# Interleaved rotary embedding: the first position of tile 0 leaves in 4 KB fp32 rows over the Activation queue

## Chip, cores, metric

The kernel runs on one core of one Trainium2 chip. The metric is device time in microseconds (us), the median of several executions. The kernel before takes 317.48 us (317.40 to 317.68, 6 runs). "Span" is the stretch that the profile covers, about 1.8 us less than the time.

## The reference

```python
# x: (8, 2048, 16, 64) fp32; cos, sin: (2048, 32) fp32
x1, x2 = x_pairs[..., 0], x_pairs[..., 1]      # even and odd elements of each head
out1 = x1 * cos - x2 * sin
out2 = x1 * sin + x2 * cos
out  = np.stack([out1, out2], axis=-1).reshape(x.shape)   # fp32
```

67.1 MB come in, 67.1 MB go out, and there are three operations on each element. Nearly everything about the time is a question of moving bytes.

## The kernel before

Each of the 8 batches is one tile: 128 partitions, 16 positions in each, 1024 elements per position. Loads and stores are issued by the Pool engine, and they change the data type on the way (a cast): fp32 in HBM, bf16 on the chip. One row (one partition of one tile) is 64 KB in HBM and 32 KB on the chip.

```python
P = 128; K = S // P; KP = 8; HEAD = 2; TAIL = 4       # K = 16; NX = NO = 3 buffers
x_t = x.rearrange("b (p k) h d -> b p k (h d)", p=P, k=K)
...
def load(b, k0=0):                       # fp32 -> bf16 in the DMA
    ...
    nc.gpsimd.dma_start(out=xs[b][:, k0:], in_=x_t[b, :, k0:])

def store(b, k1=K):                      # bf16 -> fp32 in the DMA
    nc.gpsimd.dma_start(out=out_t[b, :, :k1], in_=os[b][:, :k1])

def rotate(b, k0, k1):                   # three VectorE instructions; in short:
    ...
    o = x * c_tab;   x = x * s_tab;   o = o + x_with_neighbours_swapped

# start: positions 0 and 1 of tile 0 in fp32 over the SP and Activation queues,
# then cos and sin, then
load(0, HEAD); load(1)
...                                      # ACT casts the head, DVE builds the tables
load(2)
for b in range(B):
    os[b] = opool.tile([P, K, HD], bf16, name="ot")
    for k0 in range(0, K, KP):
        rotate(b, k0, k0 + KP)
    if b + NX < B:
        load(b + NX)
    store(b, K if b < B - 1 else K - TAIL)
...                                      # last 4 positions: cast on ACT, stored by SP
```

## Time and profile before

| what | value | where |
|---|---|---|
| time, span | 317.48 us, 315.7 us | the runs, the page |
| HBM traffic | 134.7 MB, 427 GB/s over the span | totals of the page |
| DVE (VectorE) busy | 212.8 us, 67% | busy line |
| DMA busy | 9 tenths in every slice but the last | slice rows |
| one load and one store together | 38.6 us for 16.78 MB, 434 GB/s | timeline |

From the page of the kernel before: the span, the busy line of DVE (us, share of the span, instructions), the slice rows (one digit for a 40th of the span, in tenths), and the DMA queues. The Pool queue is q0, SP's is q1, Activation's is q10; the columns are packets, MB, share of 16 engines' span.

```profile
span 315.7 us, 146 instructions
...
DVE 212.8 (67%) x51; ACT 6.9 (2%) x4; POOL 8.8 (3%) x20
...
DVE  0009999999999999619992299913999049990000
...
DMA  9999999999999999999999999999999999999996
...
q0 software_dynamic: 2304, 98.04, 97.0%
q1 hardware_dynamic: 432, 2.88, 2.4%
q10 hardware_dynamic: 288, 0.79, 0.6%
HBM read 67.63 MB, written 67.11 MB: 427 GB/s over the span
```

DVE has holes, the DMA engines have none. The DMA row is what limits the kernel.

Two pieces of the timeline of the kernel before follow (start us, us, engine, line, operation, output<-input, and in brackets how long the engine was idle and what ended that). The first piece is the end of tile 0, the second shows where tile 4 and tile 5 begin.

```profile
47.48 4.42 DVE L81 TENSOR_TENSOR ot<-ot,xt 128x8192 bf16<-128x8192 bf16 x1
51.82 4.42 DVE L75 TENSOR_TENSOR ot<-xt,c_tab 128x8192 bf16<-128x8192 bf16 x1
52.20 0.53 POOL L57 DMA_DIRECT2D xt<-in_x_dram  x1 [25.93 <-DVE ot L81]
52.72 0.54 POOL L60 DMA_DIRECT2D out_dram<-ot  x1
...
140.95 4.42 DVE L75 TENSOR_TENSOR ot<-xt,c_tab 128x8192 bf16<-128x8192 bf16 x1 [9.53 <-DMA out_dram<-ot]
...
179.53 4.42 DVE L75 TENSOR_TENSOR ot<-xt,c_tab 128x8192 bf16<-128x8192 bf16 x1 [11.98 <-DMA out_dram<-ot]
```

DVE waits until a store has left its output buffer, so these starts mark when a store landed: every 38.6 us, in which one load and one store passed.

Below the profile's views lie the records of the single DMA packets. I read from them, for the Pool queue, how far apart one engine's packets start. A packet is one row here, and the step is the time from one engine's packet start to its next. This is my own table (mean over 16 engines), not a view of the profile:

```
kernel before, Pool queue                step from packet to packet, us
loads 1 and 2 (64 KB read, 32 KB written)        2.412
last packet of load 3 -> first of store 0        3.168   (once only)
store 0 (32 KB read, 64 KB written)              2.41
later changes between load and store             2.43 to 2.45
```

65,536 bytes x 16 engines / 2.412 us is 434.7 GB/s. Loads and stores have the same step, and a load next to a store gains nothing: an engine works at the speed of the fp32 side, whether that side is read or written. The number agrees with the Trainium skill, "DMA: Bandwidth & Descriptors", section "Where 436 GB/s comes from", which gives 435.2 GB/s for the 16 ports together.

### The profile page before, as it was taken

Reading aid. Unit: us, or ns where it says so; the run is one execution under the profiler, and the core shown is the slowest. Engines: PE = TensorE matmul, PEld = TensorE weight load, DVE = VectorE, ACT = ScalarE, POOL = GpSimd, SP = SyncE. Lnnn points to the kernel's source line nnn. Section 1 sums busy time; section 2 is a strip of 40 time slices with the busy share of each in tenths; the row PEclk is TensorE's granted clock in tenths of the full one; section 3 lists DMA queues with packets and bytes.
Section 4 is the critical chain, followed back from the end, with each engine's and each line's share of the span. In section 5 each row is a group of like instructions: output and inputs, shape, how many; then the busy total and the mean of one; then the engine's idle time right before and its main releaser. Section 6 shows DMA issues by size and latency. Waiting matters only on the chain.

```text
span 315.7 us, 146 instructions
## 1 busy us (share of the span) xinstructions
DVE 212.8 (67%) x51; ACT 6.9 (2%) x4; POOL 8.8 (3%) x20
## 2 busy tenths in 40 slices
DVE  0009999999999999619992299913999049990000
ACT  2100000000000000000000000000000000000400
POOL 1000001000100100100001000000000000000000
DMA  9999999999999999999999999999999999999996
GB/s 269 212 246 203 199 212 253 199 199 237 361 465 332 199 257 407 399 332 262 203 399 440 357 199 199 482 448 266 199 316 415 399 399 523 407 399 457 423 434 280
DMA packets 3024, 101.71 MB, mean 322 GB/s; under 512 B 336, under 2 KB 336, under 8 KB 848
## 3 DMA queue, kind: packets, MB, share of 16 engines
q0 software_dynamic: 2304, 98.04, 97.0%
q1 hardware_dynamic: 432, 2.88, 2.4%
q10 hardware_dynamic: 288, 0.79, 0.6%
HBM read 67.63 MB, written 67.11 MB: 427 GB/s over the span
## 4 chain that ended last, share of the span: by engine, by line
another core or an unknown queue 61%; DMA 16%; DVE 9%; ACT 1%; issue 0%; POOL 0%; ACTq 0%
DMA out_dram<-ot 16%; DVE xt L76 3%; DVE ot L81 3%; DVE ot L75 3%; ACT xt L117 1%; DVE c_tab L100 0%; POOL xt L57 0%; ACTq L116 0%; ACT ot L116 0%; ACTq L117 0%
## 5 line engine op out<-in xcount | busy, mean ns | idle before, releaser
L75 DVE TENSOR_TENSOR ot<-xt,c_tab 128x8192 bf16<-128x8192 bf16 x16 | 70.7, 4420 | 45.8 <-DMA out_dram<-ot 45.7
L81 DVE TENSOR_TENSOR ot<-ot,xt 128x8192 bf16<-128x8192 bf16 x16 | 70.8, 4425 | 0.5
L76 DVE TENSOR_TENSOR xt<-xt,s_tab 128x8192 bf16<-128x8192 bf16 x16 | 70.8, 4425 | 0.5
L98 DVE CAST s_tab<-xt 128x512 bf16<-128x512 f32 x1 | 0.5, 454 | 23.8 <-DMA xt<-in_sin_dram 23.8
L57 POOL DMA_DIRECT2D xt<-in_x_dram x8 | 4.4, 547 | 161.4 <-DVE ot L81 137.4
L60 POOL DMA_DIRECT2D out_dram<-ot x8 | 4.3, 535 | 113.8 <-DVE ot L81 113.8
L116 ACT COPY ot<-ot 1x1 bf16<-1x1 bf16 x1 | 0.2, 193 | 286.6 <-DMA out_dram<-ot 286.6
L117 ACT CAST xt<-ot 128x4096 f32<-128x4096 bf16 x1 | 3.6, 3604 | 0.0
L96 ACT CAST xt<-xt 128x2048 bf16<-128x2048 f32 x1 | 1.9, 1897 | 0.0
L96 ACT ACT_TABLE_LOAD x1 | 1.3, 1283 | 5.7 <-DMA xt<-in_x_dram 5.7
L100 DVE CAST c_tab<-xt 128x1024 bf16<-128x1024 f32 x1 | 0.7, 683 | 0.0
L99 DVE TENSOR_SCALAR s_tab<-xt 128x512 bf16<-128x512 f32 x1 | 0.4, 442 | 0.0
L133 POOL MEMSET const-float32-0.0<- 128x1 f32 x1 | 0.1, 98 | 0.2 <-issue 0.2
L133 POOL MEMSET const-bfloat16-1.0<- 128x1 bf16 x1 | 0.1, 101 | 0.0
L133 POOL MEMSET const-float32-1.0<- 128x1 f32 x1 | 0.1, 98 | 0.0
L133 POOL MEMSET const-uint8-127<- 128x1 uint8 x1 | 0.1, 98 | 0.0
## 6 DMA issues: line engine op xcount, KB each, us to landing
xt<-in_x_dram POOLq DMA_DIRECT2D x7, 4096.0 KB, 42.8
out_dram<-ot POOLq DMA_DIRECT2D x1, 6144.0 KB, 28.0
xt<-in_x_dram POOLq DMA_DIRECT2D x1, 3584.0 KB, 22.8
out_dram<-xt SPq DMA_DIRECT2D x1, 2048.0 KB, 15.5
xt<-in_x_dram ACTq DMA_DIRECT2D x1, 512.0 KB, 5.0
xt<-in_x_dram SPq DMA_DIRECT2D x1, 512.0 KB, 4.9
xt<-in_sin_dram ACTq DMA_DIRECT2D x1, 256.0 KB, 22.7
xt<-in_cos_dram SPq DMA_DIRECT2D x1, 256.0 KB, 18.3
```

The lines of the kernel that those rows point to most:

```text
L57: nc.gpsimd.dma_start(out=xs[b][:, k0:], in_=x_t[b, :, k0:])
L60: nc.gpsimd.dma_start(out=out_t[b, :, :k1], in_=os[b][:, :k1])
L75: nc.vector.tensor_tensor(out=rows(op), in0=rows(xp), in1=tab(c_tab), op=mult)
L76: nc.vector.tensor_tensor(out=rows(xp), in0=rows(xp), in1=tab(s_tab), op=mult)
L81: nc.vector.tensor_tensor(out=o3, in0=o3, in1=x_swap, op=add)
L96: nc.scalar.copy(out=xs[0][:, :HEAD], in_=pre[:, :HEAD])
L98: nc.vector.tensor_copy(out=s2[:, :, 0], in_=sin_sb)
L99: nc.vector.tensor_scalar_mul(s2[:, :, 1], sin_sb, -1.0)
L100: nc.vector.tensor_copy(out=c_tab.rearrange("p k (i j) -> p (k i) j", j=2), in_=cos_sb.to_broadcast([P, K * D2, 2]),)
L116: nc.scalar.copy(out=os[B - 2][:1, 0, :1], in_=os[B - 1][:1, K - 1, :1])
L117: nc.scalar.copy(out=tail[:, :TAIL], in_=os[B - 1][:, K - TAIL :])
L133: nc = _bacc.Bacc("TRN2", target_bir_lowering=False, num_devices=1)
```

## The change

The intent: until 82 us, when the first packet of store 0 starts, the DMA engines only load. If the first results are ready early, a part of store 0 could leave under those loads, and store 0 would be shorter. The Activation queue is idle at that time. It gets rows that are fp32 already: ACT does the cast first.

```diff
+    LEAD = 1
+    lead = consts.tile([P, LEAD, HD], fp32)
...
-    def store(b, k1=K):
-        nc.gpsimd.dma_start(out=out_t[b, :, :k1], in_=os[b][:, :k1])
+    def store(b, k0=0, k1=K):
+        nc.gpsimd.dma_start(out=out_t[b, :, k0:k1], in_=os[b][:, k0:k1])
...
-            for k0 in range(0, K, KP):
-                rotate(b, k0, k0 + KP)
+            cuts = [0, KP, K]
+            if b == 0:
+                rotate(b, 0, HEAD)
+                nc.scalar.copy(out=lead, in_=os[b][:, :LEAD])
+                nc.scalar.dma_start(out=out_t[b, :, :LEAD], in_=lead)
+                cuts = [HEAD, KP, K]
+            for k0, k1 in zip(cuts, cuts[1:]):
+                rotate(b, k0, k1)
             if b + NX < B:
                 load(b + NX)
-            store(b, K if b < B - 1 else K - TAIL)
+            store(b, LEAD if b == 0 else 0, K if b < B - 1 else K - TAIL)
```

## The prediction

> **What bounds the kernel now.** The DMA engines, from 2 us to the end. The slice rows show DMA at 9 tenths throughout, DVE is busy 67%, and the HBM totals give 134.7 MB in 315.7 us, 427 GB/s. In the timeline the first DVE instruction of tiles 4 to 7 starts at 140.95, 179.53, 218.23 and 256.88 us, each released by a store's landing: 38.6 us for one load and one store (16.78 MB), 434 GB/s. In the single packet records each of 16 engines starts a packet (one row, 64 KB in HBM) every 2.41 us, loads and stores alike: a load beside a store gains nothing. This agrees with the Trainium skill, "DMA: Bandwidth & Descriptors", "Where 436 GB/s comes from" (435.2 GB/s). DMA issues run about 10 us ahead of their first packet (load 3 is issued at 52.2 us, its packets start near 62).
>
> **What the change removes, adds, moves.**
> - Store of tile 0: rows of 60 instead of 64 KB, 8 packets per engine: 8 x 2.41/16 = 1.21 us less on the Pool queue.
> - Activation queue: 0.5 MB more in 128 packets of 4 KB, 8 per engine. In the first load, 11 interleaved 2 KB packets per engine stretched it by 0.83 us, 0.075 us each: their bytes at 27.2 GB/s per engine, no switching cost. So 8 x 0.151 = 1.21 us, paid during loads 1 and 2. The same page, "Queues, rings and completion order", says queues take turns on an engine by packet; this trace agrees (cos and sin needed 18.3 and 22.7 us to land).
> - DVE: three instructions of 8192 elements (4.42 us) become three of 2048 and three of 6144. Estimate in proportion: 1.11 and 3.32 us, plus 0.2 us in all. Tile 0 ends near 52.2 instead of 51.9 us, so load 3 and store 0 are issued 0.2 to 0.3 us later, still ahead of need.
> - ACT: one cast of 1024 elements, about 1.04 us (estimate from 1.90 us at 2048, 3.60 at 4096), near 29 us, then one DMA issue, on an idle engine.
>
> **On the critical path.** Only the DMA terms: +1.21 - 1.21 = 0, plus one completion packet per engine (0.02 us). The intended gain, a write under a read, doesn't exist: the engines are full with loads then; work is moved, not hidden.
> One uncertainty: at the first change from loads to stores (79 to 82 us) the packets show a one-time gap of 0.6 to 1.1 us per engine, absent at later changes. If it belongs to the first HBM write, the 4 KB rows take it earlier; it may be partly hidden (-0.8 us) or happen twice (+0.8 us).
>
> **Prediction: 317.3 us, range 316.4 to 318.2.** Chances: faster by over 2% 0.01, within 2% 0.98, slower by over 2% 0.01.
>
> **What would show each step right or wrong.**
> - DMA table: Activation queue from 288 to 432 packets, 0.79 to 1.31 MB; Pool queue 0.5 MB less.
> - The 4 KB store is issued near 30 us and lands about 20 us later or more, one packet per load packet.
> - Load 2 finishes about 1.2 us later; store 0 lands near 102 us as before, within 1 us; the later DVE starts (141, 179.5, 218, 257 us) shift by under 1 us.
> - DVE busy 213.0 us; idle before the multiply still about 46 us, on stores.
>
> **What would make it wrong.** If 4 KB writes between 64 KB reads cost more than their bytes (over 0.3 us each), the time reaches 319 us. If reads and writes of an engine overlap after all, up to 1.2 us is gained. If 60 KB rows are cut into more packets, store 0 gets slower.

## The result, and the profile after

| kernel | median us | range | ratio to before | 95% interval |
|---|---|---|---|---|
| before | 317.48 | 317.40 to 317.68 | | |
| changed | 317.54 | 317.36 to 317.99 | 1.0004 | 0.9991 to 1.0017 |

The ratio is not quite the ratio of the medians.

The same lines from the page of the changed kernel:

```profile
span 316.2 us, 151 instructions
...
DVE 213.2 (67%) x54; ACT 7.9 (3%) x5; POOL 8.8 (3%) x20
...
DVE  0009999999999999619992299913999049980000
...
DMA  9999999999999999999999999999999999999996
...
q0 software_dynamic: 2304, 97.52, 96.6%
q1 hardware_dynamic: 432, 2.88, 2.3%
q10 hardware_dynamic: 432, 1.31, 1.1%
...
HBM read 67.63 MB, written 67.11 MB: 426 GB/s over the span
```

0.52 MB and no more have moved from q0 to q10, in 144 more packets (128 rows and 16 completions, packets of 4 bytes, one per engine, after the rows of a DMA). q0 still has 2304 packets: the 60 KB rows are not cut. The bytes written are the same, and so is the DMA row. (The changed kernel's profile happens to be of its slowest run, 317.99 us.)

The pieces of its timeline that answer to those of before, with the start of the new path:

```profile
27.50 1.23 DVE L83 TENSOR_TENSOR ot<-ot,xt 128x2048 bf16<-128x2048 bf16 x1
28.64 3.35 DVE L77 TENSOR_TENSOR ot<-xt,c_tab 128x6144 bf16<-128x6144 bf16 x1
28.76 1.05 ACT L112 CAST lead<-ot 128x1024 f32<-128x1024 bf16 x1 [19.94 <-DVE ot L83]
29.84 0.35 ACTq L113 DMA_DIRECT2D out_dram<-lead  x1
...
51.95 4.42 DVE L77 TENSOR_TENSOR ot<-xt,c_tab 128x8192 bf16<-128x8192 bf16 x1
52.33 0.53 POOL L59 DMA_DIRECT2D xt<-in_x_dram  x1 [26.40 <-DVE ot L83]
52.85 0.54 POOL L62 DMA_DIRECT2D out_dram<-ot  x1
...
141.18 4.42 DVE L77 TENSOR_TENSOR ot<-xt,c_tab 128x8192 bf16<-128x8192 bf16 x1 [9.63 <-DMA out_dram<-ot]
...
179.75 4.43 DVE L77 TENSOR_TENSOR ot<-xt,c_tab 128x8192 bf16<-128x8192 bf16 x1 [11.97 <-DMA out_dram<-ot]
```

The early store is issued at 29.84 us, as intended, 23 us ahead of store 0. Still the starts of tiles 4 and 5 have moved by only 0.2 us, and in the wrong direction. Nothing was gained up to there, and from there on the two kernels are alike.

The DMA view of the changed kernel shows how long the new store took (KB each, us from issue to landing):

```profile
out_dram<-lead ACTq DMA_DIRECT2D x1, 512.0 KB, 24.5
```

Half a megabyte needed 24.5 us. A window of the same view, 33 to 54 us from the start, shows why (packets, MB, share of 16 engines):

```profile
q0 software_dynamic: 150, 4.39, 97.0%
q10 hardware_dynamic: 144, 0.52, 6.6%
```

Without the 16 completions that each queue has in this window, that is 128 rows of 4 KB and 134 rows of 64 KB: each engine took about one of each in turn. The Trainium skill, "DMA: Bandwidth & Descriptors", section "Queues, rings and completion order", says that an engine takes the queues that have work in turn, by packet. That is what we see, with a single row as the unit of the turn.

What the turn costs can be read from the packet records (my table again, in us, mean over the 16 engines; the first and last lines are times between packet starts):

```
                                              before   changed
first packet of load 0 -> last of load 2       54.0     55.3     +1.4
step of a load packet, alone                   2.412    2.412
step of a load packet, with one 4 KB row         -      2.580    +0.168
last packet of load 3 -> first of store 0      3.168    3.387    +0.22 (varies)
first packet of store 0 -> first of load 4     19.3     18.1     -1.2
```

The loads give up 8 x 0.168 = 1.34 us for the 4 KB rows, and store 0 gets back 1.21 us. Net, that is +0.14 us, less than the runs can tell from zero. The one-time gap between load 3 and store 0 is still there; it differs from run to run (3.094 us in another profile of the changed kernel), so its +0.22 here says nothing about the change.

### The profile page after: what moved, and what is told of

It is laid out like the page before. It is cut to its first block, busy times and chain, and to the rows that moved or that the text cites. A ratio compares the mean times of both kernels' runs of the same rounds, so it can differ in the third digit from the quotient of the medians.

```text
span 316.2 us, 151 instructions
## 1 busy us (share of the span) xinstructions
DVE 213.2 (67%) x54; ACT 7.9 (3%) x5; POOL 8.8 (3%) x20
## 3 DMA queue, kind: packets, MB, share of 16 engines
q0 software_dynamic: 2304, 97.52, 96.6%
## 4 chain that ended last, share of the span: by engine, by line
another core or an unknown queue 61%; DMA 23%; DVE 9%; ACT 1%; issue 0%; POOL 0%; ACTq 0%; DVEq 0%
DMA out_dram<-ot 16%; DMA xt<-in_sin_dram 7%; DVE xt L78 3%; DVE ot L83 3%; DVE ot L77 3%; ACT xt L125 1%; DVE c_tab L102 0%; POOL xt L59 0%; DVE s_tab L100 0%; ACTq L92 0%; DVE s_tab L101 0%; ACT ot L124 0%; ACTq L124 0%; DVEq L77 0%
## 5 line engine op out<-in xcount | busy, mean ns | idle before, releaser
L77 DVE TENSOR_TENSOR ot<-xt,c_tab 128x8192 bf16<-128x8192 bf16 (+2 forms) x17 | 70.9, 4169 | 45.9 <-DMA out_dram<-ot 45.7
L83 DVE TENSOR_TENSOR ot<-ot,xt 128x8192 bf16<-128x8192 bf16 (+2 forms) x17 | 71.0, 4174 | 0.6
L78 DVE TENSOR_TENSOR xt<-xt,s_tab 128x8192 bf16<-128x8192 bf16 (+2 forms) x17 | 71.0, 4174 | 0.6
L112 ACT CAST lead<-ot 128x1024 f32<-128x1024 bf16 x1 | 1.0, 1046 | 19.9 <-DVE ot L83 19.9
## 6 DMA issues: line engine op xcount, KB each, us to landing
out_dram<-lead ACTq DMA_DIRECT2D x1, 512.0 KB, 24.5
```

What stands on the lines that cost most here:

```text
L77: nc.vector.tensor_tensor(out=rows(op), in0=rows(xp), in1=tab(c_tab), op=mult)
L78: nc.vector.tensor_tensor(out=rows(xp), in0=rows(xp), in1=tab(s_tab), op=mult)
L83: nc.vector.tensor_tensor(out=o3, in0=o3, in1=x_swap, op=add)
L112: nc.scalar.copy(out=lead, in_=os[b][:, :LEAD])
```

## The experiments

Theory (conservation): the DMA engines are full, so a byte costs an engine the same time wherever it is put. Rival 1 (hidden): the early write rides under the loads for nothing and is worth 1.2 us, but something else in the change, such as the cut of the arithmetic or the later issue of load 3, costs about the same. Rival 2 (lost later): what is saved at store 0 is swallowed by a later wait. All runs were timed in five rounds against the kernel before, each on the same chip as its own "before". The readings rest on the 95% intervals, about 0.13% or 0.4 us to each side.

### The changed kernel again

> The changed kernel itself, unchanged, for a reference on this chip. Conservation (a byte costs an engine the same time wherever it is put): 317.5 us, ratio 1.000 within 0.002. Rival (a write under a read is hidden, worth 1.2 us, and something else of the change costs 1.2 us): the same, so this run alone tells nothing apart.

Measured: 317.53 us against 317.46 us, ratio 1.0000 (0.9987 to 1.0012). This is the reference for the next three runs, which share its chip.

### Only the cut of the arithmetic

```diff
                 rotate(b, 0, HEAD)
-                nc.scalar.copy(out=lead, in_=os[b][:, :LEAD])
-                nc.scalar.dma_start(out=out_t[b, :, :LEAD], in_=lead)
...
-            store(b, LEAD if b == 0 else 0, K if b < B - 1 else K - TAIL)
+            store(b, 0, K if b < B - 1 else K - TAIL)
```

> Only the cut of tile 0's arithmetic into 2+6 positions; no 4 KB rows, store 0 whole. Conservation: DVE work is off the critical path, 317.5 us, ratio 1.000, DVE busy 213.2 us as in the changed kernel. Rival: this part is what costs the 1.2 us that the hidden write gives back, so 318.7 us, ratio 1.004.

Measured: 317.69 us, ratio 1.0006 (0.9994 to 1.0019), DVE busy 213.2 us. The 1.004 of rival 1 is outside the interval. The three extra DVE instructions are off the critical path.

### The first position written twice

```diff
-            store(b, LEAD if b == 0 else 0, K if b < B - 1 else K - TAIL)
+            store(b, 0, K if b < B - 1 else K - TAIL)
```

> The 4 KB rows are written over the Activation queue, and store 0 writes all 16 positions too (same values, so the result stays right; the Pool store of tile 0 waits for the early rows, which land about 1.5 us after its issue, far ahead of its first packet). Written bytes rise by 0.52 MB to 67.63 MB. Conservation: +1.21 us, 318.7 us, ratio 1.004. If the early write is hidden under the load: +0, 317.5 us. If a 4 KB packet costs more than its bytes: above +1.2 us.

Measured: 318.89 us, ratio 1.0042 (1.0028 to 1.0055), +1.43 us. The result was correct. With store 0 left whole, the early write is pure addition. It costs about its bytes (1.21 us lies in the interval of 0.9 to 1.7 us), and not nothing. Rival 1 falls.

### The first position not written at all

```diff
-                nc.scalar.copy(out=lead, in_=os[b][:, :LEAD])
-                nc.scalar.dma_start(out=out_t[b, :, :LEAD], in_=lead)
```

> Wrong on purpose: store 0 leaves out the first position and nothing writes it. Written bytes fall to 66.58 MB. Conservation: -1.21 us, 316.3 us, ratio 0.996. If the time saved at store 0 is lost again later (off the critical path, or taken by another wait): 317.5 us, ratio 1.000.

Measured: 316.45 us, ratio 0.9965 (0.9952 to 0.9977), -1.01 us; the result was wrong, as meant. What store 0 saves does arrive at the end of the kernel. Rival 2 falls.

The last four runs share a chip and the cut of the arithmetic, and differ in two things only: whether the early rows are written, and whether store 0 leaves out the first position. So each term can be read twice, with the other held fixed (medians, us):

```
                                  store 0 whole   store 0 without position 0   saved by the shorter store
no early rows                        317.69               316.45                        1.24
early rows                           318.89               317.53                        1.36
cost of the early rows                 1.20                 1.08
```

Cost and saving agree with 1.21 us within the scatter of the runs (some 0.2 us), whichever way they are taken. The line of HBM totals from the page of each of the last two kernels, first the one that writes twice, then the one that omits:

```profile
HBM read 67.63 MB, written 67.63 MB: 427 GB/s over the span
```

```profile
HBM read 67.63 MB, written 66.58 MB: 427 GB/s over the span
```

The rate is 427 GB/s in both, while the time differs by 2.4 us. The time follows the bytes.

### Two positions early

```diff
-    LEAD = 1
+    LEAD = 2
```

> Double dose: two positions leave early, in 8 KB rows. Conservation: 8 packets of 8 KB per engine, 0.302 us for their bytes and 0.017 us each as the 4 KB packets showed in the changed kernel (2.580 against 2.412 us a step, so 0.168 instead of 0.151): +2.55 us, store 0 saves 2.41 us, so 317.6 us, ratio 1.000. If the early write were hidden, -2.4 us: 315.1 us, ratio 0.992.

Measured: 317.52 us, ratio 1.0001 (0.9988 to 1.0013). Twice the dose gives the same zero, and the 0.992 of a hidden write is far outside the interval. In the packet records a load packet beside one 8 KB row has a step of 2.731 us, 0.319 us more than alone: 0.302 for the bytes and again 0.017.

### The early rows eight times

```diff
-                nc.scalar.dma_start(out=out_t[b, :, :LEAD], in_=lead)
+                for bb in range(B):
+                    nc.scalar.dma_start(out=out_t[bb, :, :LEAD], in_=lead)
```

> The same 512 KB of 4 KB rows is written eight times: to tile 0 and to the first position of tiles 1 to 7, which the later stores write over (result right; each store waits for the early rows of its tile, which should land well before). 3.67 MB more written, 56 packets of 4 KB more per engine, one beside each 64 KB packet, under loads and under stores. Conservation: 56 x 0.168 = +9.4 us over the changed kernel, 326.9 us, ratio 1.030. If a small write is hidden beside big packets: 317.5 us. If only those beside loads are hidden: about half of the 9.4.

Measured: 327.05 us, ratio 1.0297 (1.0283 to 1.0311), +9.5 us over the changed kernel (317.53 us, timed on another chip; the kernel before took 317.46 us on both) where 9.4 were expected; the result was correct. This is the cost of the early rows, made large enough to see without doubt. The step with a 4 KB row beside it is 2.580 us both in loads and in stores, so a small write is hidden neither under reads nor under other writes.

From its page:

```profile
DMA packets 4177, 105.39 MB, mean 324 GB/s; under 512 B 464, under 2 KB 464, under 8 KB 2000
...
HBM read 67.63 MB, written 70.78 MB: 425 GB/s over the span
```

3.67 MB more were written, which at 434.7 GB/s would be 8.4 us. The many small packets cost a little more than their bytes.

### The early rows over the Pool queue

The one thing I couldn't size before the run was the gap of 0.7 to 1.0 us at the first change from loads to stores, at 79 to 82 us. It is in the kernel before and in the changed one. This run asks where it belongs, and is another form of the change: no ACT cast, the DMA casts.

```diff
-                nc.scalar.copy(out=lead, in_=os[b][:, :LEAD])
-                nc.scalar.dma_start(out=out_t[b, :, :LEAD], in_=lead)
+                store(b, 0, LEAD)
```

> The first position leaves early too, but over the Pool queue with the cast in the DMA, 4 KB rows, issued near 29 us, behind loads 1 and 2. On the total both theories of the change say 317.5 us (the bytes are the same). It is for the one-time gap before the first Pool store (0.7 to 1.0 us a round of packets, in all kernels so far at 79 to 82 us). If the gap belongs to the first store of the Pool queue, it moves to near 62 us and is gone at 80. [...]

Measured: 317.08 us, ratio 0.9985 (0.9972 to 0.9997). In the packet records there is no gap at 79 to 82 us any more. At about 60 us, where the eight 4 KB rows stand between two loads, the step is 3.895 us: 2.434 as at any later change, plus 1.21 for the rows, plus about 0.25. The expectation also named what Pool issues near 78.8 us (load 4 and store 1, about 0.5 us each) as a possible cause; here Pool issues the same two at 79.16 and 79.68 us, and there is no gap. So it is tied neither to the time nor to these issues. In this run a smaller gap came with the first rows that the Pool queue stored. The rows stand together here; the first start 0.16 to 0.20 us apart, the later ones 0.153 us, which is hardly more than their bytes (0.151).

### The early rows in pieces of 512 bytes

```diff
-                nc.scalar.dma_start(out=out_t[b, :, :LEAD], in_=lead)
+                for c in range(0, HD, 128):
+                    nc.scalar.dma_start(
+                        out=out_t[b, :, :LEAD, c : c + 128], in_=lead[:, :, c : c + 128])
```

> The early rows leave as eight DMAs of 512-byte pieces: 64 small packets per engine instead of 8, the same bytes. Conservation with 0.017 us a packet: 1.21 + 64 x 0.017 = 2.30 us against 1.21 us saved, so +1.1 us, 318.6 us, ratio 1.0035, and they need about 155 us to land (one beside each 64 KB packet). If a packet costs only its bytes: 317.5 us. If it costs much more when small (0.05 us): about 320.7 us.

Measured: 318.38 us, ratio 1.0028 (1.0015 to 1.0040), +0.92 us; the last piece landed 156.1 us after its issue. The step beside one such piece is 2.448 us, 0.036 more than alone: 0.019 for the bytes and 0.017 besides. With the 4 KB and 8 KB rows this makes three sizes with the same fixed part. So it is a cost per packet squeezed in beside a long one, not a share of the bytes.

### A tiny store first, with and without a cast

If the gap belongs to the first Pool store as such, a dummy store at the start might pay it at a better time.

```diff
+    warm = consts.tile([P, 128], bf16)          # fp32 in the second of the two runs
     with tc.manual_schedule():
+        nc.vector.memset(warm, 0.0)
+        nc.gpsimd.dma_start(out=out_t[0, :, 0, :128], in_=warm)
```

Both are edits of the kernel before; store 0 writes over the zeros.

> The kernel before, with one tiny cast store (128 pieces of 512 bytes of zeros, bf16 to fp32) as the first DMA of the Pool queue, issued before the first load while the head rows keep the engines busy; store 0 writes over it. If the one-time gap belongs to the first store of the Pool queue and can be paid while the queue has nothing better to do: no gap at 79 to 82 us, 316.8 us, ratio 0.998. If the gap belongs to the first big store, or is tied to the time: the gap stays, 317.5 us or slightly more.

Measured: 317.92 us, ratio 1.0013 (0.9999 to 1.0027). The gap stays (a step of 3.180 us), and the first load is issued at 1.91 instead of 1.25 us.

> As the run before, but the tiny store is fp32 to fp32, without a cast. If what is paid once belongs to any first Pool store: gap gone, 316.8 us. If it belongs to the first store with a cast: the gap stays at 79 to 82 us, 317.5 us. (The uncast 4 KB rows of the changed kernel, on the Activation queue, did not remove it.)

Measured: 317.87 us, ratio 1.0016 (1.0003 to 1.0028), step 3.291 us. In both the gap stayed: it is not the price of the first Pool store as such. Since the gap stayed in both, whether a cast plays a part was not tested.

### The early rows over the Pool queue, repeated

> The early rows over the Pool queue once more, as a repeat: 317.1 us, ratio 0.9985. If the first reading was chance: 317.5 us, ratio 1.000.

Measured: 317.08 us, ratio 0.9991 (0.9978 to 1.0003), and the packets as in the first try. The median is the same; the interval now includes 1. The best estimate is that this form is 0.1% faster (about 0.4 us by the medians), which fits a gap that is 0.5 us smaller in the packets; more can't be said of it.

### A tiny store behind two loads

```diff
         load(0, HEAD)
         load(1)
+        nc.gpsimd.dma_start(out=out_t[0, :, 0, :128], in_=warm)
```

This too is an edit of the kernel before; `warm` is the bf16 tile of zeros as above, and its lines are left out here.

> The kernel before with the same tiny cast store of 512-byte pieces, but behind loads 0 and 1 in the Pool queue instead of ahead of all. It tells two readings of the one-time gap apart. If the gap comes at the first store that follows loads in the queue, whatever its size: a gap near 43 us (small, as the 0.25 us of the early Pool rows), none at 79 to 82 us, 317.2 us with some 0.3 us for the tiny packets. If it belongs to the first store with long rows: gap stays at 79 to 82 us, 317.8 us.

Measured: 317.66 us, ratio 1.0004 (0.9991 to 1.0018). The gap stays, with a step of 2.903 us. Following loads is not enough either: rows of 512 bytes didn't take the gap away, rows of 4 KB over the Pool queue did. What makes the gap remains open. It may be the length of the rows or the memory that they read (the three runs with a tiny store read another tile than the stores do); I haven't separated the two.

## Why the prediction was right

- **What bounds the kernel.** Right. DMA is busy from start to end in both profiles, and the time follows the written bytes: -0.52 MB gave -1.01 us, +0.52 MB gave +1.43 us, +3.67 MB gave +9.5 us over the changed kernel.
- **"+1.21 - 1.21 = 0".** Right in its mechanism. The store's side measured 1.2 us (store 0 from 19.3 to 18.1 us). The other term was a little too small: 8 x 0.168 = 1.34 us in place of 1.21.
- **"Their bytes ..., no switching cost".** Wrong by 0.017 us a packet, and the trace of before could have shown it. I divided 0.83 us by eleven packets of 2 KB, but some of those had gone ahead of the first load packet. The steps of the load beside a single 2 KB packet were longer by 0.08 to 0.095 us, and the bytes are worth 0.075. Yet the switch itself doesn't seem to be what costs: between 3 and 4 us in the same trace the 4 KB rows of the SP and Activation queues alternate on the engines, and each engine starts one every 0.155 us, 0.004 more than their bytes. The 0.017 us appear beside long rows; why is not shown.
- **DVE and ACT.** The ACT cast took 1.05 us (1.04 said), and DVE was busy 213.2 us (213.0 said). Tile 0's arithmetic took about 0.46 us longer (26.97 against 26.51 us from its first instruction to tile 1's), where 0.2 to 0.3 was said. The run with the cut alone shows that this lies off the critical path.
- **Issue and landing of the 4 KB rows.** Right: issued at 29.84 us (30 said), landed 24.5 us later (20 or more said).
- **Load 2 "about 1.2 us later", store 0 "near 102 us as before".** The last packet of load 2 started 1.3 us later (60.8 instead of 59.6 us; from the first packet of load 0 it is 1.4 us longer). Store 0 landed 0.3 us later than before, and the later DVE starts moved by 0.2 us.
- **The one-time gap.** Its two possible effects, -0.8 and +0.8 us, both failed to appear: the early rows on the Activation queue left it where it was (3.387 and 3.094 us in two profiles of the changed kernel, 3.168 before). My 317.3 leaned on a chance of a gain from it; without that lean, and with the 0.14 us of the packets, it would have been 317.6.

So 317.54 us lies inside the range of 316.4 to 318.2, 0.24 us above the point. That hit proves little by itself, since any account in which the two terms nearly cancel gives about the same total. The lean of 0.2 us to the fast side had no ground in the runs. What bears the mechanism out are the runs that show each term alone.

## What to carry to other kernels

Before moving a transfer to a "quiet" queue or an "earlier" time, ask whether the DMA engines behind all queues have free time at that moment. Where they were full, as here, the transfer was paid there in full (1.08 to 1.20 us for 0.52 MB), and only fewer bytes or fewer packets could have helped. A test that settles it at once is to do the moved transfer without taking it away from the old place, or the reverse, and better several times over: the slope tells what the work costs, where the sum of two terms tells only that they cancel. If small rows must pass beside long ones, expect what was seen here: one of them for each long row, so they landed late (24.5 us for eight rows an engine), and each cost a fixed part (0.017 us) besides its bytes.

## What the Trainium skill lacked or had wrong

- "DMA: Bandwidth & Descriptors", the warning in "Where 436 GB/s comes from", says without a condition that for transfers between HBM and SBUF the HBM limit of about 358 GB/s binds. That this is the share when both cores of a pair stream stands elsewhere, under the page's table that has 425 GB/s for 16 MB on a single core. Here a kernel on one core keeps 434.7 GB/s (64 KB for each of 16 engines per 2.412 us), so the 358 doesn't bind it; the warning lacks the condition.
- The same page, "Queues, rings and completion order", has an engine drain a packet of typically 9 to 17 descriptors before it changes queue. Here that was not so; queues changed after every single row: one 4 KB row, or one 512-byte piece, beside one 64 KB row (2.580 and 2.448 us a step).
- No page that I read has a measured time for a small packet squeezed between long ones (the same page has only a fixed overhead per packet in general). The runs show its bytes plus 0.017 us: 0.036 us for 512 bytes, 0.168 for 4 KB, 0.319 for 8 KB. The same page's "Specifications" put the least transfer for full rate at 512 bytes; in this place 512 bytes (0.019 us at 27.2 GB/s an engine) took about twice their time.
- The same page doesn't say which side sets the rate of a DMA that casts. Here it is the fp32 side: 64 KB read and 32 KB written, or the reverse, both take 2.41 us. That side is both the wider one and the one in HBM, and the runs don't separate the two.
- No page that I read has the one-time gap at the first long Pool store after loads: 0.5 to 1.0 us per engine in all kernels here but the one whose early rows of 4 KB left over the Pool queue, where about 0.25 us came with those rows instead. Its cause is open.
